# Two depth blocks of feed-forward weights interleaved in SBUF, and the gated rows set 32 bytes further apart

## The chip, the cores and the metric

The kernel runs on one core of one Trainium2 chip. The metric is the device time of one execution in microseconds (us). Before the change two timed runs gave 2304.84 and 2309.0 us, median 2306.92 us.

## What is computed

The reference is one step of a two-layer diffusion backbone over two groups of 128 tokens (a context prompt and a latent sample), 2048 features wide, in float32. Each layer is a modulated RMSNorm, an attention mixer and a residual, then another modulated RMSNorm and a gated feed-forward with a width-3 convolution over positions. The change touches the feed-forwards:

```python
D_MODEL = 2048;  D_FF = 5632
def conv_ffn(h, w_up, w_conv, b_conv, w_down):
    u = h @ w_up                                   # 2048 -> 2 * 5632
    up = jnp.pad(u, ((0, 0), (1, 1), (0, 0)))
    u = up[:, :-2] * w_conv[0] + up[:, 1:-1] * w_conv[1] + up[:, 2:] * w_conv[2] + b_conv
    gate, val = u[..., :D_FF], u[..., D_FF:]
    return (jax.nn.silu(gate) * val) @ w_down      # 5632 -> 2048
...
    x = x + gt2 * conv_ffn(h, ...)                 # in both layers
```

## The kernel before

**Layout.** Features lie on the 128 partitions, tokens along the free dimension; both token groups stand side by side, so a row of activations is NT = 256 numbers wide. A dense layer is cut into blocks of 128 input features by 128 output features. For each block TensorE loads the 128x128 block of the weight as its stationary operand (LDWEIGHTS, "PEld" in the profile) and streams the 256 tokens through it as the moving operand (MATMUL).

**Precision.** Weights and activations are float32 and are split in two: `split` (L246 to L248) writes the rounded high part with ScalarE (`wh`, L247) and the remainder with VectorE (`wl`, L248). A block then costs three matmuls of the type float32r: `wh` by the activation's high row, `wh` by its low row, `wl` by its high row. Each is a load of 128 columns and a stream of 256. `gemm` writes this loop; `first_three` does the same for the first three products of a stage, in another order.

**Weights.** The class `Weights` streams a weight from HBM in tiles `raw` of 16 blocks (8 KB per partition, one DMA of 1 MB each), splits them 8 blocks at a time into `wh` and `wl` (four buffers each, 1024 numbers or 4 KB per partition), and hands out blocks as pairs of slices. Block b of a tile is the 128 numbers from 128 b on: its columns lie 4 bytes apart, and a block begins 512 bytes behind the one before it. `chunk` hands out all the blocks of one product, `halves` and `ahead` serve the first products of a stage. The tiles are as the host has put them: `_layout` arranges every weight by blocks before the launch.

**The feed-forward.** `ffn` runs two halves (NQ = 2) for each layer. In a half, `up` makes 44 products over 16 depth blocks each (22 gates and 22 values; the moving rows are those of the tile `hx`, high and low part of a row 1024 bytes apart and rows 2048 bytes apart), convolves them (`conv`), and multiplies silu(gate) by value into 22 tiles `g`. A tile `g` holds the high row and then the low row, ROW = 512 numbers, 2048 bytes; the 22 tiles lie directly behind one another. `down` makes 16 products over these 22 depth blocks. For each layer that is 2 x 44 x 16 x 3 = 4224 matmuls up and 2 x 16 x 22 x 3 = 2112 down, for both layers 8448 up and 4224 down, 12672 together. The first products of an `up` stage (`first_three`) stream raw rows of the tile `u` or `hxc`, 258 numbers wide and so 2064 bytes apart, with the low part 1032 bytes behind the high one; a few more (`wider`) have some columns beside the 256.

**Addresses.** A few unused tiles named "pad" shift the others: `wpool` begins with one of 192 bytes, the pools of the stages with one of SHIFT = 320 bytes. As allocated, `wh` and `wl` begin 192 bytes behind a multiple of 256, `hx` and `g` 128 bytes behind one.

**Order.** The matmuls run in the order in which the tile framework's scheduler has put them; semaphores hold a product back until its `wh` and `wl` are written, and `split` until a buffer is free. The weights that are not of the feed-forwards (`w_in_ab`, `w_out_ab`, `w_in_c`, `w_out_c` and the small ones) go through the same class and the same loops.

Of the kernel before, what the change touches and what calls it, by code (L numbers as in the profile page):

```python
# [18 lines left out]
P = 128  # L19
# [74 lines left out]
def step_kernel(ctx: ExitStack, tc: tile.TileContext, A: dict):  # L94
# [157 lines left out]
    class Weights:  # L252

        def __init__(self, src, nblk, per_tile, cycle=0):
            self.src, self.nblk, self.per = src, nblk, per_tile
            self.cycle = cycle
            self.at, self.blocks, self.tiles = 0, [], []
            self.half = None  # L260
            self.begun = []
            self.used = lambda: None
# [30 lines left out]
        def halves(self, raw, lo, pin=lambda i: i, mid=None, n=8):  # L293
            wh = T_(wpool, [P, 1024], "wh", F32R, bufs=4)
            wl = T_(wpool, [P, 1024], "wl", F32R, bufs=4)
            for at in range(0, n, FINE):
                s = slice(at * P, min(at + FINE, n) * P)
                split(wh[:, s], wl[:, s], raw[:, (lo + at) * P:min(lo + at + FINE, lo + n) * P], pin)
                if mid and at == 0:
                    mid()  # L300
            return [(wh[:, b * P:(b + 1) * P], wl[:, b * P:(b + 1) * P]) for b in range(n)]

        def chunk(self):
            while len(self.blocks) < self.nblk:
                if self.half:
                    self.ahead(lambda i: i)
                    continue
                raw, n = self.take()
                n0 = FINE if fine[0] else 8
                for lo in range(0, n, n0):  # L310
                    hi = min(lo + n0, n)
                    w = (hi - lo) * P
                    if lo % 8 == 0:
                        wh_ = T_(wpool, [P, 1024], "wh", F32R, bufs=4)
                        wl_ = T_(wpool, [P, 1024], "wl", F32R, bufs=4)
                    at = lo % 8 * P
                    wh, wl = wh_[:, at:at + w], wl_[:, at:at + w]
                    split(wh, wl, raw[:, lo * P:hi * P])
                    for b in range(hi - lo):
                        s = slice(b * P, (b + 1) * P)  # L320
                        self.blocks.append((wh[:, s], wl[:, s]))
                    self.tiles += [(wh_, wl_)] if lo % 8 == 0 else []
                self.used()
            out, self.blocks = self.blocks[:self.nblk], self.blocks[self.nblk:]
            return out
# [1153 lines left out]
    def ffn(hx, W, ready, turn, l, st):  # L1479
        xh, xl = (lambda k: hx[:, k, :NT]), (lambda k: hx[:, k, NT:2 * NT])  # L1480
        wider = list(WIDER)
        long = len(ready) > 3

        def product():
            if ready:
                return ready.pop(0)
            if in_order:
                return gemm(W.chunk(), xh, xl, between=in_order.pop(0))
            if wider:
                n = NT + wider.pop(0)  # L1490
                return gemm(W.chunk(), xh, xl, more=lambda k: hx[:, k, :n])
            return gemm(W.chunk(), xh, xl)

        WD = Weights(A["w_down"][l], KQ, TB)
        cw = ada["cw"]
        with tc.tile_pool(name=f"ffn{l}", bufs=1) as fp, banks(f"pffn{l}") as pf:
            feat["home"], feat["pool"] = fp, pf
            feat["due"] = 0.0
            in_order = [{}, {}] + turn + [{}]
            T_(fp, [P, SHIFT // 4], "pad")  # L1500

            def conv(m):
                early = bool(ready)
                pin = keep_order if early else lambda i: i
                if len(ready) > 4 - 2 * long:
                    W.ahead(pin)
                ps = product()
                y = T_(fp, [P, NT], "cv", bufs=3)
                pin(act.activation(y, ps, AF.Identity, scale=cw[:, 1, m:m + 1], bias=cw[:, 3, m:m + 1]))  # L1509
                y3 = y.rearrange("p (g t) -> p g t", g=2)  # L1510
                p3 = ps.rearrange("p (g t) -> p g t", g=2)
                pin(dve.scalar_tensor_tensor(out=y3[:, :, 1:], in0=p3[:, :, :T - 1],  # L1512
                                             scalar=cw[:, 0, m:m + 1], in1=y3[:, :, 1:],
                                             op0=ALU.mult, op1=ALU.add))
                pin(dve.scalar_tensor_tensor(out=y3[:, :, :T - 1], in0=p3[:, :, 1:],  # L1515
                                             scalar=cw[:, 2, m:m + 1], in1=y3[:, :, :T - 1],
                                             op0=ALU.mult, op1=ALU.add))
                if early and ready and not long:
                    W.ahead(pin)
                return y  # L1520

            def up(q):
                gs = []
                for i in range(q * KQ, (q + 1) * KQ):
                    rate = 0 if i < LATE else FRATE["up"]
                    fine[0] = False
                    gate = conv(i)
                    pump(0, rate)
                    val = conv(NFF + i)
                    pump(0, rate)  # L1530
                    act.activation(gate, gate, AF.Silu)
                    dve.tensor_tensor(out=val, in0=gate, in1=val, op=ALU.mult)
                    g = T_(fp, [P, ROW], "g", F32R, bufs=KQ)
                    split(g[:, :NT], g[:, NT:2 * NT], val)
                    gs.append(g)
                    if i == LATE - 1:
                        load_row()
                return gs

            def down(gs, q):  # L1540
                u, rows = None, None
                if q == NQ - 1 and l < NL - 1:
                    u = raw_tile(keep, "hx")
                    rows = raw_rows(u, l + 1, 0)
                for c in range(KD):
                    quiet = q == NQ - 1 and c >= KD - QUIET[0]
                    fine[0] = quiet
                    if q == 0:
                        ensure(l, 5, [c // 4])
                    ps = gemm(WD.chunk(), lambda k: gs[k][:, :NT], lambda k: gs[k][:, NT:2 * NT])  # L1550
                    if l == NL - 1 and q == NQ - 1 and c == KD - 1:
                        last_residual(ps, l, 1, c, st)
                    else:
                        residual(ps, l, 1, c, st if q == NQ - 1 else None)
                    if rows:
                        rows(c)
                    if l == NL - 1 and q == NQ - 1 and c in EARLY:
                        act.activation(x[:, c], x[:, c], AF.Identity, scale=C("gfin")[:, c:c + 1])
                    pump(0, 0 if quiet else FRATE["down"])
                return u  # L1560

            for q in range(NQ):
                gs = up(q)
                u = down(gs, q)
            while feat["i"] < FLIMIT[stage[0]]:
                feature_step()
            return u


    with banks("pab") as ppool["ada"]:  # L1570
# [11 lines left out]
        with tc.tile_pool(name="beside", bufs=1) as beside:  # L1582
            o = mixer_ab(hx, beside)
            with tc.tile_pool(name="raw", bufs=1) as rp:
                T_(rp, [P, SHIFT // 4], "pad")
                u = raw_tile(rp, "u")
                out_ab(o, st, u, beside, rp)
                W = Weights(A["w_up"][0], KD, 1)
                hx, *begun = modulated(st, 0, 1, W, u, (keep, "hx"), rp)
    stage[0] = "ffn0"  # L1590
    st = stat_init()
# [2 lines left out]
    with tc.tile_pool(name="cc", bufs=1) as cp, banks("pc") as ppool["ada"]:  # L1594
        ada["pool"] = cp
        ppool["att"] = ppool["ada"]
        T_(cp, [P, SHIFT // 4], "pad")
        W = Weights(A["w_in_c"], KD, 1)
        hx, *begun = modulated(st, 1, 0, W, u, (cp, "hxc"), cp, "dev")
        load_cw(1)  # L1600
        st = stat_init()
        ada["pew"] = PEW["c"]
        u = mixer_c(cp, hx, W, begun[0], st)
        W = Weights(A["w_up"][1], KD, 1)
        hx, *begun = modulated(st, 1, 1, W, u, (keep, "hx"), cp, "dev")
    stage[0] = "ffn1"
    st = stat_init()
# [53 lines left out]
def _layout(i):  # L1661
# [46 lines left out]
    for h in range(0, 8, 2):  # L1708
# [11 lines left out]
    a["w_down"] = np.stack([  # L1720
        _tiles(*(_blocks(i["w_ffn_down"][l][q * KQ * P:(q + 1) * KQ * P], range(KD), 1)
                 for q in range(NQ))) for l in range(NL)])
    return {n: np.ascontiguousarray(v) for n, v in a.items()}


# [30 lines left out]
```

## Time and profile before

| What | Value |
|---|---|
| Timed runs, median | 2306.92 us |
| The profiled execution, own time | 2304.7 us |
| Its span, first to last instruction | 2302.9 us |
| Mean granted TensorE clock | 0.996 of full |
| TensorE, matmuls (PE) | busy 2272.1 us, 99% of the span, 19528 records |
| TensorE, weight loads (PEld) | busy 2180.0 us, 95% |
| VectorE / ScalarE / GpSimd | 82% / 52% / 8% |
| First feed-forward, steady part | about 471 to 1162 us |
| Second feed-forward, steady part | about 1575 to 2290 us |

Matmuls overlap in the profile: a record lasts about 276 ns, while the next one starts about 113 ns later. So neither the mean duration nor the busy share tells how fast the stream runs; what tells it is the distance from one start to the next, which is the length of an uninterrupted stretch divided by its number of matmuls. It is called the **pitch** below.

### The profile page before, as it was taken

How to read it: one execution, taken by the hardware profiler on the slowest of the kernel's cores; microseconds unless marked ns; L12 is line 12 of the kernel's file. 1: busy time of each engine (PE TensorE's matmuls, PEld its weight loads, DVE VectorE, ACT ScalarE, POOL GpSimd, SP SyncE). 2: the span in 40 equal slices, each digit the busy share in tenths (PEclk: the TensorE clock that was granted, in tenths of full speed). 3: DMA queues.
4: the chain of work that ended last, by engine and by line, in shares of the span. 5: the costliest groups of instructions: out<-in, count | busy, mean ns of one | idle time of the engine just before them, and what ended most of it. 6: DMA issues, size and time to landing. Idle time of an engine off the chain costs nothing.

```text
span 2302.9 us, 47585 instructions
## 1 busy us (share of the span) xinstructions
PE 2272.1 (99%) x19528; PEld 2180.0 (95%) x19528; DVE 1886.1 (82%) x2973; ACT 1199.3 (52%) x1975; POOL 188.2 (8%) x238
## 2 busy tenths in 40 slices
PE   8899989999999999999999999999999999999998
PEld 6788868999999999999999999999999999999998
DVE  4668979889989999999988988898899965666654
ACT  4346555665554355555575455457555434555543
POOL 0012111300000000001130001023000000000011
PEclk9999999999999999999999999999999999999999
DMA  9988879777767777777787888776677755555553
GB/s 386 374 334 305 329 291 359 290 275 250 272 259 288 286 276 262 260 273 256 284 304 290 311 309 324 259 273 230 245 254 264 263 201 188 199 192 193 198 189 127
DMA packets 100122, 617.15 MB, mean 268 GB/s; under 512 B 10752, under 2 KB 18880, under 8 KB 33344
## 3 DMA queue, kind: packets, MB, share of 16 engines
q1 hardware_dynamic: 99904, 614.11, 72.0%
q8 instruction: 153, 2.51, 0.4%
q14 instruction: 65, 0.53, 0.1%
HBM read 609.32 MB, written 4.75 MB: 267 GB/s over the span
## 4 chain that ended last, share of the span: by engine, by line
PE 96%; DMA 2%; DVE 1%; ACT 1%; issue 0%; SPq 0%; POOL 0%; DVEq 0%; ACTq 0%; POOLq 0%
PE acc L109 89%; PE ada L109 3%; PE att L109 2%; PE att L112 1%; DMA raw<-w_in_ab 1%; DVE wl L248 1%; DMA kvb<-w_ada 0%; DMA araw<-w_ada 0%; PE misc L109 0%; ACT wh L247 0%; PE ada L112 0%; DVE hx L520 0%; DVE x L1616 0%; DVE qb L1138 0%; ACT p L870 0%
## 5 line engine op out<-in xcount | busy, mean ns | idle before, releaser
L109 PE MATMUL acc<-hx,wh 128*128 128x256 f32 (+1 forms) x7264 | 1252.4, 278 | 5.0 <-ACT wh L247 1.7
L247 ACT CAST wh<-raw 128x1024 fp32r<-128x1024 f32 (+1 forms) x834 | 796.6, 967 | 878.8 <-PE acc L109 745.7
L248 DVE TENSOR_TENSOR wl<-raw,wh 128x1024 fp32r<-128x1024 f32 (+1 forms) x834 | 924.4, 1124 | 248.2 <-ACT wh L247 243.3
L109 PEld LDWEIGHTS acc<-hx,wh 128*128 128x128 f32 x7264 | 1097.3, 188 | 23.8 <-issue 8.9
L109 PE MATMUL acc<-hx,wl 128*128 128x256 f32 (+1 forms) x3632 | 1005.7, 277 | 6.3 <-DVE wl L248 6.1
L109 PEld LDWEIGHTS acc<-hx,wl 128*128 128x128 f32 x3632 | 682.9, 188 | 10.5 <-DVE wl L248 7.9
L109 PE MATMUL acc<-g,wh 128*128 128x256 f32 x2816 | 478.8, 276 | 0.0
L109 PEld LDWEIGHTS acc<-g,wh 128*128 128x128 f32 x2816 | 423.8, 188 | 0.0
L109 PE MATMUL acc<-g,wl 128*128 128x256 f32 x1408 | 388.0, 276 | 0.0
L468 DVE CUSTOM_DVE_ANT_0 junk<-araw,condb 128x2048 f32<-128x2048 f32 x128 | 294.1, 2297 | 0.0
L109 PE MATMUL acc<-hxc,wh 128*128 128x256 f32 (+1 forms) x1568 | 282.7, 282 | 0.0
L109 PEld LDWEIGHTS acc<-g,wl 128*128 128x128 f32 x1408 | 264.1, 188 | 0.0
L109 PEld LDWEIGHTS acc<-hxc,wh 128*128 128x128 f32 x1568 | 241.3, 189 | 4.6 <-issue 4.2
L109 PE MATMUL acc<-hxc,wl 128*128 128x256 f32 (+1 forms) x784 | 218.4, 279 | 0.0
L210 POOL TENSOR_TENSOR sqacc<-sqacc,sq 128x256 f32<-128x256 f32 x62 | 71.5, 1154 | 1490.7 <-ACT sq L206 1490.4
L109 PEld LDWEIGHTS acc<-hxc,wl 128*128 128x128 f32 x784 | 147.5, 188 | 0.4
L1509 ACT ACTIVATE cv<-acc,convw 128x256 f32<-128x256 f32 x169 | 94.2, 558 | 0.0
L520 DVE CUSTOM_DVE_ANT_0 hx<-block,condb 128x1024 fp32r<-128x1024 f32 x65 | 79.2, 1218 | 7.4 <-DMA block<-w_ada 6.8
L1515 DVE SCALAR_TENSOR_TENSOR cv<-acc,convw,cv 128x254 f32<-128x254 f32 x169 | 80.8, 478 | 3.2
L838 DVE SCALAR_TENSOR_TENSOR x<-acc,mod,x 128x128 f32<-128x128 f32 x190 | 57.1, 342 | 31.7 <-PE acc L109 31.7
L1512 DVE SCALAR_TENSOR_TENSOR cv<-acc,convw,cv 128x254 f32<-128x254 f32 x169 | 80.1, 474 | 0.0
L109 PE MATMUL ada<-araw,condw 128*32 128x512 f32 (+1 forms) x608 | 75.7, 585 | 0.8 <-DMA araw<-w_ada 0.8
(263 smaller groups left out, 1532.9 us busy)
## 6 DMA issues: line engine op xcount, KB each, us to landing
raw<-w_up SPq DMA_DIRECT2D x176, 1024.0 KB, 4.8
araw<-w_ada SPq DMA_DIRECT2D x136, 1024.0 KB, 6.2
raw<-w_down SPq DMA_DIRECT2D x88, 1024.0 KB, 4.8
raw<-w_in_c SPq DMA_DIRECT2D x48, 1024.0 KB, 6.8
block<-w_ada SPq DMA_DIRECT2D x41, 512.0 KB, 6.6
raw<-w_in_ab SPq DMA_DIRECT2D x18, 1024.0 KB, 9.2
raw<-w_out_ab SPq DMA_DIRECT2D x16, 1024.0 KB, 8.2
raw<-w_out_c SPq DMA_DIRECT2D x16, 1024.0 KB, 6.5
```

Source lines behind the costliest of these rows:

```text
L109: return self.placed(nc.tensor.matmul(*a, **kw))
L112: return self.placed(nc.tensor.transpose(*a, **kw))
L210: eng.tensor_tensor(out=st["acc"], in0=st["acc"], in1=sq, op=ALU.add)
L247: pin(act.copy(out_hi, src))
L248: pin(dve.tensor_tensor(out=out_lo, in0=src, in1=out_hi.bitcast(F32), op=ALU.subtract))
L468: keep_order(dve.tensor_tensor_reduce(out=T_(feat["pool"], [P, D], "junk"), in1=feat["row"][:, c], in0=feat["raw"].rearrange("p g n -> p ( ...
L520: keep_order(dve.tensor_tensor_reduce(out=self.junk, in0=self.raw, in1=self.row[:, c].rearrange("p (g n) -> p g n", g=2), scale=1.0, scala ...
L838: dve.scalar_tensor_tensor(out=x[:, c, s], in0=ps[:, s], scalar=mod[:, l, 3 * which + 2, c, g:g + 1], in1=x[:, c, s], op0=ALU.mult, op1=AL ...
L1509: pin(act.activation(y, ps, AF.Identity, scale=cw[:, 1, m:m + 1], bias=cw[:, 3, m:m + 1]))
L1512: pin(dve.scalar_tensor_tensor(out=y3[:, :, 1:], in0=p3[:, :, :T - 1], scalar=cw[:, 0, m:m + 1], in1=y3[:, :, 1:], op0=ALU.mult, op1=ALU.add))
L1515: pin(dve.scalar_tensor_tensor(out=y3[:, :, :T - 1], in0=p3[:, :, 1:], scalar=cw[:, 2, m:m + 1], in1=y3[:, :, :T - 1], op0=ALU.mult, op1=A ...
```

## The change

Three things change.

1. The host writes the weights `w_up` and `w_down` of both layers so that in each pair of depth blocks the columns alternate: column m of the first block, column m of the second, column m + 1 of the first, and so on. A block's 128 columns then lie 8 bytes apart over 1024 bytes; the second block of the pair begins 4 bytes behind the first, and the next pair 1024 bytes behind this one. The number of bytes and of DMAs stays.
2. `Weights` gets a flag `mixed`, set for these weights alone, and a function `block` that hands out such a strided slice in place of a contiguous one. `split` works on whole runs of columns, as before, so ScalarE and VectorE read and write the same contiguous stretches; only LDWEIGHTS reads with a stride. All 12672 matmuls of the feed-forwards, and no others, have such a load.
3. The tiles `g` are 8 numbers longer, ROW + 8 = 520, so that the 22 gated rows lie 2080 bytes apart in place of 2048. Modulo 256 bytes, each row begins 32 bytes further than the one before it, and the ninth where the first did. Rows of `hx` stay 2048 bytes apart.

The instructions, their order on every engine and their waits stay what they were, apart from line numbers; only addresses and the stride of the stationary operand differ.

```diff
-        def __init__(self, src, nblk, per_tile, cycle=0):
+        def __init__(self, src, nblk, per_tile, cycle=0, mixed=False):
+            self.mixed = mixed
             self.src, self.nblk, self.per = src, nblk, per_tile
...
-            return [(wh[:, b * P:(b + 1) * P], wl[:, b * P:(b + 1) * P]) for b in range(n)]
+            return [(self.block(wh, b), self.block(wl, b)) for b in range(n)]
+
+        def block(self, w, b):
+
+            if not self.mixed:
+                return w[:, b * P:(b + 1) * P]
+            return w.rearrange("p (g m i) -> p g i m", i=2, m=P)[:, b // 2, b % 2]
...
-                    for b in range(hi - lo):
-                        s = slice(b * P, (b + 1) * P)
-                        self.blocks.append((wh[:, s], wl[:, s]))
+                    for b in range(lo % 8, lo % 8 + hi - lo):
+                        self.blocks.append((self.block(wh_, b), self.block(wl_, b)))
...
-        WD = Weights(A["w_down"][l], KQ, TB)
+        WD = Weights(A["w_down"][l], KQ, TB, mixed=True)
...
-                    g = T_(fp, [P, ROW], "g", F32R, bufs=KQ)
+                    g = T_(fp, [P, ROW + 8], "g", F32R, bufs=KQ)
...
-                W = Weights(A["w_up"][0], KD, 1)
+                W = Weights(A["w_up"][0], KD, 1, mixed=True)
...
-        W = Weights(A["w_up"][1], KD, 1)
+        W = Weights(A["w_up"][1], KD, 1, mixed=True)
...
+    for n in ("w_up", "w_down"):
+        a[n] = a[n].reshape(*a[n].shape[:-1], -1, 2, P).swapaxes(-1, -2).reshape(a[n].shape)
     return {n: np.ascontiguousarray(v) for n, v in a.items()}
```

## The prediction

> **What bounds the kernel now.** The page first: the engines' busy time, and the chain of work that ended last.
>
> ```profile
> PE 2272.1 (99%) x19528; PEld 2180.0 (95%) x19528; DVE 1886.1 (82%) x2973; ACT 1199.3 (52%) x1975; POOL 188.2 (8%) x238
> ...
> PE 96%; DMA 2%; DVE 1%; ACT 1%; issue 0%; SPq 0%; POOL 0%; DVEq 0%; ACTq 0%; POOLq 0%
> ```
>
> TensorE carries 96% of the chain. Next, two stretches of the view of windows: the first feed-forward without its edges, and most of the second mixer.
>
> ```profile
> core 0: us, PE busy (x) PEld busy (x) DVE busy (x) ACT busy (x) POOL busy (x), PEclk, DMA share, GB/s
> 520.00:1150.00 630.00, 630.00 (x5561) 630.00 (x5560) 588.93 (x756) 316.44 (x436) 15.67 (x13) 1.00 0.73 270
> ...
> 1180.00:1500.00 320.00, 319.58 (x2690) 304.86 (x2683) 276.29 (x475) 172.40 (x340) 26.95 (x40) 1.00 0.82 301
> ```
>
> In the feed-forward TensorE never stops, at a granted clock of 1.00, and 630 us / 5561 matmuls give a pitch of 113.3 ns. No weights, rows or buffers are waited for there: the largest wait between ScalarE or VectorE and TensorE is the other way round.
>
> ```profile
> ACT wh L247 <- PE acc L109: 745.7, 523, 5.5
> ```
>
> ScalarE sat idle for 745.7 us, 523 times, until TensorE gave a `wh` buffer free. So the time of a feed-forward is its number of matmuls by the pitch, and the question is what makes the pitch. The timeline of 0.3 us there shows both of TensorE's rows.
>
> ```profile
> 1701.84 0.19 PEld L109 LDWEIGHTS acc<-hx,wl 128*128 128x128 f32 x1
> 1701.95 0.28 PE L109 MATMUL acc<-hx,wl 128*128 128x256 f32 x1
> 1701.96 0.30 PEld L109 LDWEIGHTS acc<-hx,wh 128*128 128x128 f32 x2
> 1702.07 0.39 PE L109 MATMUL acc<-hx,wh 128*128 128x256 f32 x2
> 1702.18 0.19 PEld L109 LDWEIGHTS acc<-hx,wl 128*128 128x128 f32 x1
> ```
>
> A matmul starts 0.11 us after its load; the next load starts 0.01 us or less after that matmul. Together that is the pitch: load and stream take turns, the load of the next block runs beside the stream of this one, and the matmul cannot start before its load is through. Whatever lengthens a load's reading lengthens the pitch by as much; that is where the change acts.
>
> How much of the 113.3 ns is the load by itself? Where a matmul has one column, hardly anything is streamed beside the loads:
>
> ```profile
> 1161.75 0.36 PE L109 MATMUL att<-cst,sq 128*128 128x1 f32 x2
> 1161.98 0.36 PE L109 MATMUL att<-cst,sqacc 128*128 128x1 f32 x2
> 1162.20 0.36 PE L109 MATMUL att<-cst,sq 128*128 128x1 f32 x2
> 1162.42 0.36 PE L109 MATMUL acc<-hx,wh 128*128 128x258 f32 x1
> ```
>
> Six loads of 128 columns in 1162.42 - 1161.75 = 0.67 us, 111.7 ns each. The stream of 256 beside the load therefore costs only 1.6 ns in the feed-forward. It costs more elsewhere, as the chain in order of time shows for pieces without a pause:
>
> ```profile
> 440.57 3.23 PE acc L109 x27
> ...
> 1203.76 11.31 PE acc L109 x96
> ...
> 1215.40 5.47 PE acc L109 x48
> ```
>
> In the second mixer, with rows of 256 at the same alignments, one piece has 11.31 / 96 = 117.8 ns and the next 5.47 / 48 = 114.0 ns. The piece at 440 us is a product on raw rows of 258 columns that drift by 2064 bytes from row to row: 3.23 / 27 = 119.6 ns, or 118.7 ns scaled to 256 columns. So the same instructions run at a short pitch (113.3), at a long one (117.8), and at something above that when the two streams' positions keep changing. Two reads of SBUF by one engine evidently disturb each other, depending on where they stand. The feed-forwards keep the short pitch nearly throughout.
>
> **The change part by part.** How many matmuls it touches follows from the loops: 8448 up and 4224 down; the latter stand in the page.
>
> ```profile
> L109 PE MATMUL acc<-g,wh 128*128 128x256 f32 x2816 | 478.8, 276 | 0.0
> L109 PEld LDWEIGHTS acc<-g,wh 128*128 128x128 f32 x2816 | 423.8, 188 | 0.0
> L109 PE MATMUL acc<-g,wl 128*128 128x256 f32 x1408 | 388.0, 276 | 0.0
> ```
>
> 2816 + 1408 = 4224, each with its load. So 1 ns of pitch is 12.7 us over both parts, 8.4 us up and 4.2 us down.
>
> *Nothing else moves.* The same instructions stand in the same order on all engines, each DMA has the same bytes, `split` writes the same contiguous runs, and 22 x 32 bytes more of SBUF fit. Were the pitch the same, the time would be too. Cover for a small gain is there: VectorE, the busiest of the others, has 588.93 of 630 us in the first window, 93%.
>
> *The strided loads.* No load in this trace has a stride, so the price needs bounds. Below: a load that the stream doesn't disturb, 111.7 ns in place of 113.3, a gain of 1.6 x 12.672 = 20 us. Above: the price of a column comes from the loads of 32 columns,
>
> ```profile
> L109 PEld LDWEIGHTS ada<-araw,condw 128*32 128x32 f32 x608 | 15.6, 110 | 24.7 <-issue 18.5 <-DMA araw<-w_ada 1.0
> ```
>
> (188 - 110) / 96 = 0.81 ns a column. If 8 bytes of step halved that rate, a load would grow by 128 x 0.81 = 104 ns and the kernel by 1.3 ms. I take the lower end's neighbour, no loss: the weights would cover 8 / 0.81 = 9.9 bytes of a row per ns and the stream 256 x 4 / 110 = 9.3, so the strided load covers its 1024 bytes at the pace at which the stream, which does not stall, covers its own.
>
> [...]
>
> *The rows of `hx`.* They stay 2048 bytes apart and a pair of weight blocks 1024: every load meets its stream at the same relative place, but for 4 bytes. Until now the weights covered 512 bytes while the stream covered 1024, so that the places slid past each other within each load; now they run abreast. That can hold the reads apart for good or hold them together. Bounds: -1.6 and +5.4 ns (118.7, the drifting rows) for 8448 matmuls, -14 to +46 us. I take 0: the nearest row is that of the same tile with a fixed distance, 113.3.
>
> *The rows of `g`.* Here the fixed distance goes: each row begins 32 bytes further. The bounds are the same two, -7 to +23 us for 4224 matmuls. The nearest rows are those that drift; but the raw rows also begin off a multiple of 16 bytes every other time (1032 bytes from high to low), which `g` never does, so I take the long pitch, 117.8: 4.5 x 4.224 = 19 us.
>
> **Sum.** Against the profiled execution's 2304.7 us (span 2302.9 and 1.8 around it): 0 + 0 + 19 = 2323.7 us; the median of the timed runs lies 2.2 us higher, so 2326 us, +0.8%.
>
> **The rivals.**
>
> *The long pitch on both sides (slower).* Streams that run abreast stay in conflict for the whole load once they begin in one: every load pays what it pays at the long pitch, 4.5 x 12.672 = 57 us, 2364 us, and at the drifting rows' pitch 5.4 x 12.672 = 68 us, 2375 us. It passes 2% when the mean pitch rises by 46 / 12.672 = 3.6 ns. For it: the stretch at 1203 us keeps the long pitch for 96 matmuls without falling out, and the weights now fetch twice as many places, with no slack between them. Against: one delay of a few ns would move the abreast streams apart. Chance 0.25.
>
> *Line-bound loads (far slower).* The stride costs the load itself: anything from 10 ns a load, 127 us, up to the 1.3 ms above. For it: the load is what the matmul waits for, with nothing to hide it. Chance 0.09.
>
> *Free loads (a small gain).* Abreast and apart, the loads run as beside one-column matmuls: -20 us, 2287 us. For it: 111.7 ns is seen in the trace. Chance 0.18.
>
> *Nothing at all.* Neither stride nor distance matters; `g` stays quick: 2307 us. Against it speak the two pitches, which come with the same shapes and clock. Chance 0.16. [...]
>
> *A gain over 2%.* It needs 109.7 ns, below the load alone, 111.7; nothing in the trace with 128 plain columns gets there. Chance 0.04.
>
> **How the numbers follow.** That leaves 0.28 for the forecast and its surroundings (2312 to 2345), the likeliest single case. Within 2% (2261 to 2353, about what a measurement of this kernel can tell from no change): 0.28 + 0.18 + 0.16 = 0.62, less 0.02 for a forecast that comes out worse, 0.60. Slower: 0.25 + 0.09 + 0.02 = 0.36. Faster: 0.04. The range goes from the free loads, 2287 less 3 us, to the drifting rows' pitch on both sides, 2375 and 3 us: 2284 to 2378. Outside are the line-bound loads, the large gain and some of the edges, 0.17 or so.
>
> **What would show it.** In the changed profile, the matmuls of 520 to 1150 us counted again: the `hx` stretches should keep 5561 in 630 us less what `g` loses, a `g` stretch alone should have 117 to 118 ns. In the timeline the load should still start at most 0.01 us after the matmul, and the matmul 0.11 us after its load; more there is the load's reading. Waits for `wh` and `wl` should stay away from TensorE. The forecast is wrong if `hx` products change by more than 2 ns, if `g` is as quick as before, or if PEld records grow from 188 ns by tens of ns.

## The result, and the profile after

The changed kernel takes 2390.64 us (2390.38 to 2390.89) against 2306.92 us before: a ratio of 1.0363, 95% interval 1.0318 to 1.0407. It is slower by 83.7 us. The time lies 13 us above the upper end of the predicted range and 65 us above the forecast.

The page of the changed kernel, in the lines on the engines' busy time and on the chain that ended last, reads nearly as before:

```profile
PE 2357.5 (99%) x19528; PEld 2265.6 (95%) x19528; DVE 1893.1 (79%) x2973; ACT 1195.9 (50%) x1975; POOL 189.6 (8%) x238
...
PE 95%; DMA 2%; DVE 2%; issue 0%; ACT 0%; SPq 0%; POOL 0%; DVEq 0%; ACTq 0%; POOLq 0%
```

TensorE is the bound in both, with the same 19528 matmuls and 85 us more of busy time. The other engines have the same instructions and a smaller share of a longer span. Two stretches of the view of windows (number of records in brackets) tell where the time is: the same one of the first feed-forward, and the stretch of the second mixer that holds the work of 1180 to 1500 us before. It lies 44 us later now, because the first feed-forward takes longer.

```profile
core 0: us, PE busy (x) PEld busy (x) DVE busy (x) ACT busy (x) POOL busy (x), PEclk, DMA share, GB/s
520.00:1150.00 630.00, 630.00 (x5250) 630.00 (x5249) 558.25 (x704) 296.73 (x399) 10.67 (x7) 1.00 0.70 255
1224.00:1544.00 320.00, 319.42 (x2684) 304.49 (x2677) 275.76 (x476) 171.81 (x337) 25.58 (x40) 1.00 0.82 300
```

In the feed-forward 630 us held 5561 matmuls before and hold 5250 now: 120.0 ns each in place of 113.3, at a granted clock of 1.00. In the second mixer, whose weights are not interleaved, 320 us hold 2684 matmuls where they held 2690, 119.2 ns each in place of 119.0. So the loss is in the feed-forwards. It is in both of their parts, as two shorter windows show, one inside `up` (rows of `hx`) and one inside `down` (rows of `g`). First the kernel before:

```profile
480.00:660.00 180.00, 180.00 (x1589) 180.00 (x1589) 165.38 (x213) 99.61 (x137) 0.00 (x0) 1.00 0.71 258
730.00:800.00 70.00, 70.00 (x620) 70.00 (x620) 64.30 (x73) 27.10 (x26) 0.00 (x0) 1.00 0.79 293
```

and the changed one:

```profile
480.00:660.00 180.00, 180.00 (x1502) 180.00 (x1501) 155.38 (x200) 93.83 (x128) 0.00 (x0) 1.00 0.66 241
730.00:800.00 70.00, 70.00 (x584) 70.00 (x584) 61.83 (x74) 25.29 (x25) 0.00 (x0) 1.00 0.76 278
```

180 us / 1502 = 119.8 ns with `hx` and 70 us / 584 = 119.9 ns with `g` (a count includes one or two matmuls that only overlap an edge; over all distances between starts in the trace the means are 120.0 and 120.2). Before, these means were 113.4 and 113.3. That is the loss: 12672 matmuls by 6.6 ns, the few wider streams counted alike, are 84 us, and 83.7 were measured.

No wait of TensorE has come with it: it waits 7.1 us in all for `wh` and `wl`, where it waited 7.8. The largest wait between TensorE and the two engines that split the weights is still that of ScalarE for a free weight buffer, and it has grown from 745.7 us:

```profile
ACT wh L247 <- PE acc L109: 835.2, 536, 5.5
```

In the groups of the page the records themselves are longer, each load by 8 ns and each matmul by 7 ns, with no idle time ahead of them (last column):

```profile
L109 PE MATMUL acc<-g,wh 128*128 128x256 f32 x2816 | 507.8, 283 | 0.0
L109 PEld LDWEIGHTS acc<-g,wh 128*128 128x128 f32 x2816 | 445.5, 196 | 0.0
```

And in the timeline of a `hx` stretch (start, length, engine, line, operation, operands) load and matmul take turns as before:

```profile
599.91 0.40 PE L109 MATMUL acc<-hx,wh 128*128 128x256 f32 x2
599.91 0.19 PEld L109 LDWEIGHTS acc<-hx,wh 128*128 128x128 f32 x1
600.03 0.19 PEld L109 LDWEIGHTS acc<-hx,wl 128*128 128x128 f32 x1
600.15 0.28 PE L109 MATMUL acc<-hx,wl 128*128 128x256 f32 x1
```

A load starts together with the matmul before its own; its own matmul follows 0.12 us later (loads at 599.91 and 600.03, the matmul of the second at 600.15), where it was 0.11. What has grown is the time from a load's start to its matmul.

### The profile page after: what moved, and what is told of

It reads as the page before. It is cut to its first block, busy times and chain, and to the rows that moved or that the text cites. A ratio compares the mean times of both kernels' runs of the same rounds, so it can differ in the third digit from the quotient of the medians.

```text
span 2389.1 us, 47585 instructions
## 1 busy us (share of the span) xinstructions
PE 2357.5 (99%) x19528; PEld 2265.6 (95%) x19528; DVE 1893.1 (79%) x2973; ACT 1195.9 (50%) x1975; POOL 189.6 (8%) x238
## 3 DMA queue, kind: packets, MB, share of 16 engines
q1 hardware_dynamic: 99904, 614.11, 69.6%
## 4 chain that ended last, share of the span: by engine, by line
PE 95%; DMA 2%; DVE 2%; issue 0%; ACT 0%; SPq 0%; POOL 0%; DVEq 0%; ACTq 0%; POOLq 0%
PE acc L109 89%; PE ada L109 3%; PE att L109 2%; DMA kvb<-w_ada 1%; PE att L112 1%; DMA raw<-w_in_ab 1%; DVE wl L248 1%; DMA block<-w_ada 0%; PE misc L109 0%; PE ada L112 0%; DVE hx L526 0%; DVE x L1622 0%; ACT wh L247 0%; SPq L966 0%; DVE hx L248 0%
## 5 line engine op out<-in xcount | busy, mean ns | idle before, releaser
L109 PE MATMUL acc<-hx,wh 128*128 128x256 f32 (+1 forms) x7264 | 1307.8, 282 | 4.7 <-ACT wh L247 1.7
L109 PEld LDWEIGHTS acc<-hx,wh 128*128 128x128 f32 x7264 | 1136.3, 193 | 23.3 <-issue 8.5
L109 PE MATMUL acc<-hx,wl 128*128 128x256 f32 (+1 forms) x3632 | 1025.1, 282 | 5.6 <-DVE wl L248 5.4
L109 PEld LDWEIGHTS acc<-hx,wl 128*128 128x128 f32 x3632 | 698.6, 192 | 9.8 <-DVE wl L248 7.2
L109 PE MATMUL acc<-g,wh 128*128 128x256 f32 x2816 | 507.8, 283 | 0.0
L109 PEld LDWEIGHTS acc<-g,wh 128*128 128x128 f32 x2816 | 445.5, 196 | 0.0
L109 PE MATMUL acc<-g,wl 128*128 128x256 f32 x1408 | 397.2, 283 | 0.0
L109 PEld LDWEIGHTS acc<-g,wl 128*128 128x128 f32 x1408 | 275.9, 196 | 0.0
```

Of the source, the lines that this page charges most:

```text
L109: return self.placed(nc.tensor.matmul(*a, **kw))
```

## The experiments

Three causes could stand behind the 6.6 ns. **The load itself** ((B) in the expectations below): 128 columns 8 bytes apart take longer to read, whatever streams beside them. **Conflict** ((A) below): the load now covers 1024 bytes in the time in which the stream covers 1024, and the two disturb each other; that is the mechanism of the rival "the long pitch on both sides", and it should depend on the place of the one against the other and be gone where nothing is streamed. **The rows of `g`**, which drift. In what follows the *place* is the address at which a block of weights begins less that of the row, modulo 256 bytes: 64 in the kernel before (192 less 128).

### The rows of g alone

```diff
-                    g = T_(fp, [P, ROW], "g", F32R, bufs=KQ)
+                    g = T_(fp, [P, ROW + 8], "g", F32R, bufs=KQ)
```

Against the kernel before; the weights stay contiguous.

> The 22 gated rows 2080 bytes apart, no weight interleaved. The two theories: (A) the interleaved columns make the whole loss, by the loads' reads meeting the stream's more often; (B) the loads alone are slower with a step of 8 bytes; both leave this kernel to the rows' distance alone. If the distance costs what drifting rows cost in the profile before (117.8 to 118.7 ns in place of 113.3), 4224 matmuls give +19 to +23 us: 2326 to 2330 us. If it costs nothing without the interleaving, 2307 us. The up products stay at 113.4 ns in either case.

Measured: 2344.82 us against 2308.1, ratio 1.0157 (1.0140 to 1.0174), 36.7 us slower. Three windows of this kernel: in the first `up` half, in the `down` after it, in the second `up` half.

```profile
520.00:640.00 120.00, 120.00 (x1062) 120.00 (x1061) 111.33 (x145) 64.12 (x89) 0.00 (x0) 1.00 0.71 258
740.00:800.00 60.00, 60.00 (x513) 60.00 (x512) 53.68 (x60) 22.08 (x21) 0.00 (x0) 1.00 0.79 290
820.00:1000.00 180.00, 180.00 (x1530) 180.00 (x1530) 161.06 (x207) 92.21 (x129) 0.00 (x0) 1.00 0.69 252
```

The first `up` half keeps the short pitch (120 us / 1062 = 113.0 ns). The `down` with the drifting rows has 60 / 513 = 117.0, over all its matmuls 117.6 ns: 4.3 ns more than before, 18 us for 4224 of them. The third row was not foreseen: 180 / 1530 = 117.6 ns for the second `up` half, which has the same instructions at the same kind of addresses as the first. It begins right behind the stretch at 117.6 ns and keeps its own pitch to its end; the second layer does the same, 113.7 ns in the first half over all starts and 117.8 in the second. Half of the 8448 `up` matmuls at 4.5 ns more are 19 us, and 18 + 19 = 37 us is the measured loss. So one set of addresses has two pitches, and here the long one came behind a slower stretch. That the slower stretch was the cause is not shown.

### The interleaved weights alone

```diff
-                    g = T_(fp, [P, ROW + 8], "g", F32R, bufs=KQ)
+                    g = T_(fp, [P, ROW], "g", F32R, bufs=KQ)
```

This is the changed kernel with its third part undone.

> Weights interleaved, gated rows 2048 bytes apart as before. By (A) and (B) the up products stay at the changed kernel's 120 ns. By (A), with rows at a fixed distance, the down products fall into the up products' rhythm, 120 ns, and the time stays at 2391 us within 5. Had the distance made the down products' loss, they return to 113.4 ns: 4224 x 6.8 = 29 us less, 2362 us.

Measured: 2389.28 us against 2308.1, ratio 1.0352 (1.0337 to 1.0368). The windows in `up` and in `down`:

```profile
480.00:660.00 180.00, 180.00 (x1502) 180.00 (x1502) 155.33 (x201) 92.77 (x127) 0.00 (x0) 1.00 0.66 240
730.00:800.00 70.00, 70.00 (x585) 70.00 (x585) 61.93 (x71) 25.34 (x25) 0.00 (x0) 1.00 0.77 280
```

They read as those of the whole change, in `down` too (585 against 584), where the rows now do not drift. The interleaving by itself makes nearly the whole loss, and the two parts do not add up: 37 us and 81 us by themselves, 84 us together. With strided loads there is no short pitch left for the drifting rows to spoil.

### Load against stream, without the kernel around them

A small program issues nothing but matmuls, 192 of one kind in a row, out of eight blocks in SBUF, with nothing awaited; it computes none of the reference. Its core:

```python
for i in range(192):
    k = i % 8
    nc.tensor.matmul(ps[:, :cols], bl[k], x, start=i == 0, stop=i == 191)
# bl: blocks of 128 columns with a step of s numbers, w.rearrange("p (m i) -> p i m", i=s)[:, i]
```

> A kernel without the model's work: 192 matmuls for each of 34 cases, rows and blocks in SBUF from the start; its outputs are left at zero. By (A) a load of 128 columns beside a stream of 32 columns takes 111 to 112 ns a matmul with plain columns and the same with a step of 8 bytes; beside a stream of 256 it is 113 to 118 plain and about 120 with the step. By (B) the step costs some 6 to 7 ns beside 32 columns too, 118. Steps of 16 and 32 bytes put each column on another 16 bytes: by (A) only a little more than 120 beside a stream and 112 alone, by (B) far more, up to twice the load (215 ns). [...] With the step of 8 bytes at ten relative places: by (A) some place is clearly better (113 or less) or worse than others; by (B) all alike.

The timeline, one row for each kind (`beside4x`: a load with a step of 4 numbers beside a stream of 256; `long`, `half`, `two0`: streams of 512, 128, 256; `moved2x`: a plain load and a stream whose own columns have a step of 2 numbers). The pitch of a kind is the distance from its start to that of the next row, divided by 192.

```profile
223.35 23.21 PE L62 MATMUL ps<-beside2x,wt 128*128 128x256 f32 x192
246.40 45.39 PE L62 MATMUL ps<-beside4x,wt 128*128 128x256 f32 x192
291.62 46.49 PE L62 MATMUL ps<-beside8x,wt 128*128 128x256 f32 x192
337.95 44.95 PE L62 MATMUL ps<-long1x,wt 128*128 128x512 f32 x192
382.74 44.33 PE L62 MATMUL ps<-long2x,wt 128*128 128x512 f32 x192
...
472.67 21.55 PE L62 MATMUL ps<-half1x,wt 128*128 128x128 f32 x192
494.05 22.78 PE L62 MATMUL ps<-half2x,wt 128*128 128x128 f32 x192
516.67 23.26 PE L62 MATMUL ps<-two0x,wt 128*128 128x256 f32 x192
...
861.13 44.32 PE L62 MATMUL ps<-moved2x,wt 128*128 128x256 f32 x192
905.25 21.98 PE L62 MATMUL ps<-again1x,wt 128*128 128x256 f32 x192
927.07 23.20 PE L62 MATMUL ps<-again2x,wt 128*128 128x256 f32 x192
```

| Step of the load's columns | Beside a stream of 256 | Beside 128 | Beside 512 |
|---|---|---|---|
| 4 bytes | 113.6 ns (`again1x`) | 111.4 | 233.3 |
| 8 bytes | 120.0 | 117.8 | 230.1 |
| 16 bytes | 235.5 | not run | 238.3 |
| 32 bytes | 241.3 | not run | not run |

The 120.0 ns of the changed kernel stand here with no other engine at work. Ten places with a step of 8 bytes, 0 to 224, gave 119.1 to 121.1 ns: the place hardly matters, which speaks against conflict. Halving the stream takes 2.2 ns off and leaves 6.4 ns of difference between 8 and 4 bytes. Beside 512 columns, where the stream needs longer than either load, the step of 8 bytes costs nothing (230.1 ns, 233.3 with plain loads). And the stream has a price of the same kind: with an 8-byte step of its own columns it takes (905.25 - 861.13) / 192 = 229.8 ns, twice the plain one's 113.6. The loads with next to no stream that this program also held ran at a granted clock of 0.50 and can't be set beside the others directly (the last section says what they show); the next program puts such loads between dense stretches.

### The load alone

```diff
-SECTIONS += [(f"alone{s}x", s, 32, 64, 1) for s in (1, 2, 4, 8)]
+SECTIONS += [(f"few{c}s{s}x", s, c, 64, 0, "all", 12) for c in (2, 32, 64) for s in (1, 2, 4)]
+SECTIONS += [(f"n{c}s{s}x", s, c, 64, 0, "all", 0) for c in (96, 160, 192, 224, 248, 256, 264, 288)
+             for s in (1, 2)]
...
```

This program, too, computes none of the reference. `few2s2x` is a load with a step of 2 numbers beside a stream of 2 columns, 24 of them between 72 plain matmuls of 256, twelve times over; `n264s1x` is a row of 192 plain loads beside streams of 264. Further rows go through more places, `even` and `odd` blocks apart, and drifting against fixed rows.

> A kernel without the model's work again, outputs left at zero; short stretches (24 matmuls) with hardly any stream stand between dense ones, so that the granted clock stays at 1.00. (A) The step of 8 bytes costs only where the stream's reads are met: beside streams of 2, 32 and 64 columns 111 to 112 ns with and without the step, then rising with the stream's length to 117.8 at 128 and 120 at 256. (B) The step brings the loads to the limit of what their own reads deliver: 116 to 118 ns already beside 2 columns, flat up to 128, and only the last 2 ns to 120 come with the stream. Step of 16 bytes beside 2 columns: (A) 112 to 118, (B) about 220. Even and odd blocks alone: alike within 1 ns by both; if the 4 bytes mattered, one of them 113. Plain columns at other relative places: 117 to 120 but for 64, and neighbours of 64 by 4 or 8 bytes show how narrow that place is. Rows drifting by 32 bytes: 117 to 118 plain, 120 with the step, as in the full kernels.

The timeline, first the loads that stand alone:

```profile
169.27 2.73 PE L67 MATMUL ps<-few2s1x,wt 128*128 128x2 f32 x24
171.86 8.73 PE L67 MATMUL ps<-warm,wt 128*128 128x256 f32 x72
180.43 2.88 PE L67 MATMUL ps<-few2s2x,wt 128*128 128x2 f32 x24
183.16 2.09 PE L67 MATMUL ps<-warm,wt 128*128 128x256 f32 x12
```

From the first row to the second are 2.59 us for 24 loads, from the third to the fourth 2.73: 0.14 us more, 5.8 ns a load. Start by start, over all twelve repetitions, a plain load takes 111.7 ns (the prediction's figure) and one with a step of 8 bytes 117.8, beside 2, 32 or 64 streamed columns alike; with 16 bytes it takes 233.3. The view of windows gives a granted clock of 1.00 for 169.2 to 171.9 us and for 180.4 to 183.2 us, where the two pieces lie; the single loads are alike in all repetitions, and the plain one agrees with that of the kernel before. This settles the disputed term: **the load itself takes 6.1 ns longer**, with hardly a stream to conflict with.

Then streams of growing length, and single places for plain loads at the end:

```profile
1747.89 22.77 PE L67 MATMUL ps<-n256s1x,wt 128*128 128x256 f32 x192
1770.50 23.20 PE L67 MATMUL ps<-n256s2x,wt 128*128 128x256 f32 x192
1793.54 23.23 PE L67 MATMUL ps<-n264s1x,wt 128*128 128x264 f32 x192
1816.61 23.20 PE L67 MATMUL ps<-n264s2x,wt 128*128 128x264 f32 x192
...
1890.85 23.21 PE L67 MATMUL ps<-even2x,wt 128*128 128x256 f32 x192
1913.89 23.20 PE L67 MATMUL ps<-odd2x,wt 128*128 128x256 f32 x192
1936.93 23.14 PE L67 MATMUL ps<-evenhalf2x,wt 128*128 128x128 f32 x192
1959.91 22.71 PE L67 MATMUL ps<-one16x,wt 128*128 128x256 f32 x192
...
2051.26 21.94 PE L67 MATMUL ps<-one64x,wt 128*128 128x256 f32 x192
2073.04 22.35 PE L67 MATMUL ps<-one68x,wt 128*128 128x256 f32 x192
```

Beside 264 columns a plain load and a strided one both come to 120 ns (23.07 and 23.04 us / 192), beside 288 both to 133.3: there the stream is the longer of the two and hides the step. At 256 columns the strided load gives 23.04 / 192 = 120.0 ns for even and for odd blocks, and the plain one 113.4 at place 64 (`one64x`). The plain one also gave 117.8 at that place (`n256s1x`), where the stretch began behind slower ones: the two pitches again. Other places give plain loads 115.6 (68 bytes) to 121.7 ns (56). Drifting rows cost a plain load 5.0 ns (118.4 against 113.4) and a strided one 0.6 (120.6 against 120.0), which fits that the two parts of the change do not add up. Beside 128 columns the strided loads of the even blocks alone (`evenhalf2x`) give 22.98 / 192 = 119.7 ns, where those of all eight blocks gave 117.8 in the program before.

### Another place for hx, weights as before

```diff
-    T_(wpool, [P, 48], "pad", bufs=1)
+    T_(wpool, [P, 32], "pad", bufs=1)
```

All `wh` and `wl` begin 64 bytes earlier; `hx` is then at place 0, the other tiles, moved along, stay at 64.

> The kernel before with the first pad of the weights' pool 64 bytes shorter: weights and rows of hx then begin at the same place modulo 256 bytes (64 bytes apart before), while the distance to g, hxc and the raw rows stays at 64, since their pools lie behind and move along. No interleaving, no other distance between rows. If the short pitch of 113.3 ns hangs on the place, the up products go to what plain columns show at place 0 in the kernel of streams, 120 ns: 8100 x 6.6 = 53 us, and a few more for the first mixer, 2360 to 2368 us; the down products may follow or stay at 113.4. If the short pitch comes from the plain columns alone, 2307 us.

Measured: 2372.37 us against 2307.93, ratio 1.0277 (1.0260 to 1.0294). The windows in `up` and in `down`:

```profile
480.00:660.00 180.00, 180.00 (x1503) 180.00 (x1502) 156.26 (x203) 94.17 (x130) 0.00 (x0) 1.00 0.67 244
730.00:800.00 70.00, 70.00 (x620) 70.00 (x619) 66.59 (x79) 26.97 (x26) 0.00 (x0) 1.00 0.80 300
```

With contiguous loads and 64 bytes of difference `hx` has 180 / 1503 = 119.8 ns, as after the change, and `g` has the short pitch, 70 / 620 = 112.9. So the 113.3 ns of the kernel before belong to its place. The time came out 4 to 12 us above what was expected. Most of that lies in the first mixer, which streams rows of `hx` too: there the pitch went from 115.0 to 119.8 ns for some 1700 matmuls, 8 us, where the expectation had counted a few us. Over all 4224 matmuls of `down` the mean is 113.35 ns: they took up the short pitch although an `up` at 120 ns ran ahead of them.

### Four blocks interleaved

```diff
-            return w.rearrange("p (g m i) -> p g i m", i=2, m=P)[:, b // 2, b % 2]
+            return w.rearrange("p (g m i) -> p g i m", i=4, m=P)[:, b // 4, b % 4]
...
-        a[n] = a[n].reshape(*a[n].shape[:-1], -1, 2, P).swapaxes(-1, -2).reshape(a[n].shape)
+        a[n] = a[n].reshape(*a[n].shape[:-1], -1, 4, P).swapaxes(-1, -2).reshape(a[n].shape)
```

The rows of `g` are as before the change. A block's columns lie 16 bytes apart.

> Four depth blocks interleaved in place of two, so a block's columns lie 16 bytes apart; gated rows 2048 bytes apart. If a load is paid by the pieces of 16 bytes that it touches (32 pieces hidden behind 128 columns: 111.7 ns; 64 pieces 117.8; 128 pieces 233 alone and 235.5 beside a stream of 256 in the kernels of streams), the 12672 matmuls of the feed-forwards go from 113.4 to 235.5 ns: 122.1 x 12.672 = 1547 us more, 3855 us. If the loss of the change is the meeting of the two reads and not the load itself, a load that still asks for one column in 0.83 ns stays near 120 ns: 2390 to 2450 us.

Measured: 3852.37 us against 2308.22, and in one window:

```profile
600.00:900.00 300.00, 300.00 (x1276) 300.00 (x1275) 138.36 (x172) 76.41 (x107) 0.00 (x0) 1.00 0.35 125
```

300 us / 1276 = 235.1 ns, the small program's 235.5. The price that the small programs gave carries over to the kernel: 12672 x (235.1 - 113.3) ns = 1543 us, measured 1544.

### Is the short pitch to be had elsewhere?

The second mixer has a mean pitch of 115.4 ns over `hxc`, above the 113.3 of the feed-forwards. Its matmuls are interrupted more often (from 1203 to 1222 us its chain consists of pieces of 96 and 48 with others between them), so a third small program (none of the reference in it) breaks groups of 48 plain matmuls by three others, at 20 places.

> Streams of 256 beside plain loads, in groups of 48 that three float32 matmuls break, as in the mixers; 16 relative places and four neighbours of 64; the model's work left out, outputs zero. If place 64 gives the short pitch only when a group happens to begin well, its groups mix 113.3 and 117.8 ns, about 115 to 116 in the mean as in the second mixer, and the other places stay at 117 to 120. A place with less than 114 in the mean would be worth trying in the mixers.

The groups of its trace (matmuls, then busy time in us and mean ns of one record), for two places of 576 matmuls each and for place 64 with 1152:

```profile
L60 PE MATMUL ps<-p64x,wt 128*128 128x256 f32 x1152 | 139.2, 280 | 0.0
...
L60 PE MATMUL ps<-p0x,wt 128*128 128x256 f32 x576 | 72.0, 285 | 0.0
...
L60 PE MATMUL ps<-p192x,wt 128*128 128x256 f32 x576 | 68.7, 278 | 0.0
```

Per 576 matmuls place 64 needs 69.6 us, place 192 needs 68.7 and place 0 needs 72.0. At place 64, which was run in two turns of twelve groups, those of the first turn keep the short pitch (43 or 44 of 47 distances are below 115.5 ns) and those of the second the long one throughout; at 192 ten of the twelve groups keep the short one. So place 192 was no better than place 64 in its better turn. Two kernels try that place with contiguous weights and rows as before. In the first the pool of the second mixer moves:

```diff
-        T_(cp, [P, SHIFT // 4], "pad")
+        T_(cp, [P, SHIFT // 4 + 32], "pad")
```

> The kernel before with the pad of the second mixer's pool 128 bytes longer: the rows of hxc then stand at the relative place 192 in place of 64, all else as before. In the streams broken every 48 matmuls, place 192 held the short pitch for most of its matmuls where place 64 held it for a third to a half. If the mixer follows, its 2127 matmuls of 256 columns on hxc go from 115.4 to about 114 ns, 3 us less, 2305 us and a little under the kernel before; if its breaks (transposes, matmuls of 32 weights) begin the groups otherwise, nothing or up to 117.8 ns, 5 us more.

Measured: 2310.29 us against 2306.77, ratio 1.0013 (1.0004 to 1.0022), a little slower. The window of the second mixer, 2690 matmuls before:

```profile
1180.00:1500.00 320.00, 319.57 (x2656) 305.11 (x2649) 273.31 (x469) 169.13 (x331) 22.98 (x39) 1.00 0.82 298
```

The pitch over `hxc` rose from 115.4 to 117.2 ns. In the second the weights move, so that `hx` is at place 192:

```diff
-    T_(wpool, [P, 48], "pad", bufs=1)
+    T_(wpool, [P, 16], "pad", bufs=1)
```

> The kernel before with the first pad of the weights' pool 128 bytes shorter: the rows of hx, in the first mixer and in both up products, stand at place 192, while g, hxc and the raw rows stay at 64. An unbroken stream at 192 kept 117.8 ns in one kernel of streams, broken ones were mostly at 113.3. If the up products keep the short pitch, 2305 to 2308 us; if they begin in the long one, they stay in it as in the kernel with the rows' distance alone: 8100 x 4.5 = 36 us more, 2343 us. The down products, at place 64, either inherit the long pitch (another 19 us) or stay at 113.4.

Measured: 2349.26 us against 2306.77, ratio 1.0187 (1.0173 to 1.0201). Windows in the first `up` half and in `down`:

```profile
520.00:640.00 120.00, 120.00 (x1021) 120.00 (x1020) 106.52 (x138) 61.20 (x87) 0.00 (x0) 1.00 0.70 256
740.00:800.00 60.00, 60.00 (x532) 60.00 (x531) 56.33 (x65) 23.22 (x22) 0.00 (x0) 1.00 0.80 289
```

120 / 1021 = 117.5 ns: the long pitch throughout `up`. The `down` behind it is at the short one at once (60 / 532 = 112.8), so a long pitch is not always inherited either. What the small program showed for place 192 did not carry over to the kernel, and no version beat the kernel before. Why, of the places tried, only 64 keeps the short pitch in long stretches, and what decides between the two, stays open.

## Why the prediction was wrong

**What bounds the kernel** held: TensorE carries the chain (95% of it after the change), load and matmul take turns, and the time is the number of matmuls by the pitch. That 1 ns is worth 12.7 us over 12672 matmuls held as well (84 / 6.6). That **nothing else moves** held: the second mixer counts 2684 matmuls for 2690 in the same stretch of work, and TensorE's waits for `wh` and `wl` did not grow (7.1 us, 7.8 before).

**"The strided loads" is the step that failed.** It put the term at 0, which no run shows: the load by itself grew from 111.7 to 117.8 ns, 6.1 ns or 77 us, and what the pitch has above that beside a stream of 256 grew from 1.6 to 2.2 ns, the other 7 us. The working compared the pace of the load in bytes covered, 9.9 per ns, with that of the stream, 9.3, and concluded that the load would not stall. Both paces were read from lengths that do not give them. The 0.81 ns a column came from the lengths of records, which overlap; the prediction's own 111.7 ns for 128 columns are 0.87 ns, so the strided load would have had to cover 9.2 bytes per ns, while a stream of 1024 bytes in a pitch of 113.3 ns covers 9.0. By these figures the load was asked to be faster than the stream that it was held against. The runs give 1024 / 117.8 = 8.7 bytes per ns for the strided load and 2048 / 233.3 = 8.8 for a stream of 512 columns, so the idea that the two have like paces was right, but not that this pace costs the load nothing. The plain load needed only 512 bytes in its 111.7 ns, and with no load of the 12672 hidden, those 6.1 ns come in full: the timeline has 0.12 us from a load's start to its matmul where it had 0.11. An argument good to a tenth was used for a sum in which 2% of the kernel's time are 3.6 ns.

**"The rows of `hx`"**, also 0, had an upper bound of 5.4 ns from the drifting rows. `hx` rose by 6.6 ns in the mean over the starts of `up` (113.4 to 120.0), outside that bound: the bound was taken from plain loads, and a longer load was no part of it. The 2.2 ns beyond the load's 117.8 do not go by the place (ten places within 2 ns), nor by even against odd blocks (120.0 both). Beside 128 columns they are absent with all eight blocks (117.8) but there with the even ones alone (119.7), so not even the stream of 256 is shown to make them. What they are is not settled, nor whether it is more than chance that the strided load has the same 117.8 ns as the long pitch of plain ones.

**"The rows of `g`"**, 4.5 ns and 19 us, was right in size by itself: 4.3 ns and 18 us without the interleaving. That a row which begins off a multiple of 16 bytes costs more for it, the ground for 117.8 in place of 118.7, no run shows: places off such a multiple gave plain loads 115.6 to 121.7 ns, places on one 113.4 to 119.9. Two things were missed. Beside strided loads the drift costs next to nothing more (84 us with it, 81 without, each against its own runs of the kernel before), so the terms don't add. And without them the kernel loses twice the term, 37 us, since the second `up` half runs at the long pitch too.

**The rivals.** "The long pitch on both sides" had the sign, both sides, and nearly the size (2364 to 2375), with a chance of 0.25. Its mechanism, streams abreast in conflict, fell: a load beside 2 columns is as long as beside 64 (117.8 ns). That its size came near was a coincidence of two prices. In kind it was "line-bound loads", the step costing the load itself, whose lower end of 10 ns was too high by 4; the forecast gave nothing to the gap between the two. "Free loads" and "nothing at all" fell by the counts of `hx` and `g`.

**The signs named** worked in part. The criterion of `hx` changing by over 2 ns told at once that the forecast was wrong. The PEld records grew by 5 to 8 ns (188 to 193 in the group of `hx`, which holds the first mixer too, and to 196 with `g`), below the "tens of ns" that were to show a longer load, and the timeline's steps of 0.01 us were as large as the effect (0.11 to 0.12).

## What to carry to other kernels

Where every matmul waits for its own load, and load and stream are within a few ns of each other, a stationary operand should be contiguous: two blocks interleaved cost 6.6 ns in 113 here and four cost 122, while beside streams of 264, 288 and 512 columns the step of 8 bytes was free (120.0 ns for 120.2, 133.3 for 133.3, 230.1 for 233.3). A pitch that is repeated 12672 times is best priced by such a short program of one kind of matmul, or by counting matmuls in an uninterrupted window, since busy shares and mean durations hardly show it. The relative place of stationary and moving operand was worth 4 to 7 ns a matmul in float32r in the two kernels that moved the weights, and a layout that is moved for another reason can lose that.

## What the runs showed of the hardware

- **A price that goes by the step.** At a granted clock of 1.00 a load of 128 columns costs 111.7 ns with a step of 4 bytes (512 bytes covered), 117.8 with 8 (1024 bytes) and 233.3 with 16 (2048 bytes). Beside a stream of 256 columns, steps of 16 and 32 bytes are nearly alike, 235.5 and 241.3. Beside plain loads, a stream that covers 1024 bytes costs 113 to 122 ns, one of 1152 bytes (288 columns) 133.3, one of 2048 bytes 233.3 as 512 plain columns and 229.8 as 256 columns with a step. From 1024 to 2048 bytes that is 233.3 - 117.8 = 115.5 ns for the load and 229.8 - 113.6 = 116.2 for the stream. The pieces of 16 bytes in an expectation above are the author's estimate: the doubling from 8 to 16 bytes of step and the 5.8 ns from 16 to 32 fit them, but no run shows such a unit by itself.
- **Two pitches at the same place**, 113.3 and 117.8 ns, each lasting for some 2000 matmuls: with the rows of `g` alone, the first `up` half kept the short one and the second the long one over the same tile `hx`. What decides which one comes is not settled.
- **The clock, and what does not follow it.** Loads beside streams of 32 columns ran at a granted clock of 0.50 in the first small program, though TensorE was never idle. Its windows for a step of 4, 8 and 16 bytes:

```profile
38.00:66.00 28.00, 28.00 (x133) 28.00 (x133) 0.00 (x0) 0.00 (x0) 0.00 (x0) 0.50 0.00 1
68.00:108.00 40.00, 40.00 (x189) 40.00 (x189) 0.00 (x0) 0.00 (x0) 0.00 (x0) 0.50 0.00 0
109.00:152.00 43.00, 43.00 (x186) 43.00 (x186) 0.00 (x0) 0.00 (x0) 0.00 (x0) 0.50 0.00 1
```

From start to start these are 213.3, 213.3 and 233.3 ns; between dense stretches, at 1.00, they were 111.7, 117.8 and 233.3. The plain load takes nearly twice as long at half the clock, the load with a step of 16 bytes just as long, and the step of 8 bytes costs nothing there. An estimate that fits these six numbers to 5 ns: a load takes the longer of two times, one that goes by the granted clock (213.3 / 2 = 106.7 ns at 1.00, 0.83 ns a column) and one that the step sets and the clock does not change (117.8 and 233.3 ns). That is a second sign that the step costs the load its own reading, and no conflict. The price of an 8-byte step in a small program, 0 ns at 0.50 and 6.1 at 1.00, came near the kernel's 6.6 only at a granted clock like the kernel's.
